# A decoder block on one core: first down-projection loads asked for in the last gate/up unit, residual added in the second group, last group in another order

## Chip, cores and metric

The kernel runs on one core of a Trainium2 chip. The metric is the device time of one execution in microseconds (us); the runs shown are three executions of the kernel before, and one more execution was profiled.

## What is computed

One hybrid decoder block in float32 on 1024 tokens of width 1024: a norm, an input projection, a state-space mixer and a retention mixer side by side, an output projection with a residual, and then the part that the change touches:

```python
h = rmsnorm(x, norm2_w[i])
a = jax.nn.silu(jnp.einsum("bsd,df->bsf", h, w_gate[i]))
u = jnp.einsum("bsd,df->bsf", h, w_up[i])
x = x + jnp.einsum("bsf,fd->bsd", a * u, w_down[i])
...
return rmsnorm(x, final_norm_w)
```

The inner width is 2816, which is 22 blocks of 128 or 11 pairs of blocks.

## The kernel before

Every float32 operand is split in two parts (`split`: ScalarE writes the rounded part, VectorE the rest), and each product is three TensorE matmuls of 128x128 by 128x512. The gate, up and down projections are done by Strassen's scheme in Winograd's form: two by two blocks need seven products, numbered 1 to 7, and each product goes into an accumulator in PSUM that several products share.

**Gate and up.** There are 22 units (class `Unit`), gate and up in turn for the 11 pairs. A unit runs its products in the order of `ORDER`, `(1, 5, 6, 2, 7, 3, 4)`; the first six units (`EARLY`) have done 1 and 2 beforehand and run `(5, 6, 7, 3, 4)`. The string `"XXYZYZZ"[i - 1]` names the accumulator of product i: 5 and 3 go to Y, and 6, 7 and 4 go to Z. After 5 and after 6 the accumulator is read out (`L989`: the tile `RS` for 6), before a later product is added on top. After the second unit of a pair, seven combinations of the result are split and stored to DRAM (`down_op`, `L1027`, tensors `aD`) through three staging buffers (the tile `x7` and two halves of `ktok`).

**Down.** The 11 pairs are taken in three groups of 4, 4 and 3 (`down_proj`), and each group runs seven products (class `Down`), one step for each pair in the group, 12 matmuls a step. The string `"1Z 5Y 6Z 3Y 7Z 2Y 4Z"` gives product and accumulator set (four PSUM banks each, one for each 128 tokens). A step needs two things: the stored combinations (`a`, loaded from `aD`, `L1160`) and a weight operand (`w`) made from raw rows of `w_down`: an even block (tile `qk`) and an odd block (tiles `m8` to `m11`), loaded at `L1152`. Product 5 makes a difference `t` of the halves of the even block, and later products change `t` with the odd block. `a` and `w` rotate over 20 tiles, `RING`: `m0`-`m3`, `m4`-`m7`, `h4`-`h7`, `m12`-`m15`, `h0`-`h3`. In gate/up these same tiles, with `qk`, hold the operands `B[1]` to `B[7]` of products 1 to 7: `B[1]` in `qk`, `B[5]` in `m0`-`m3`, `B[6]` in `m4`-`m7`, `B[2]` in `h4`-`h7`, `B[7]` in `m8`-`m11`, `B[3]` in `m12`-`m15` and `B[4]` in `h0`-`h3`.

After the last step of each product, `evac` adds each bank to its part of the result (`L1219`), tiles `x3[h, t]` (h a half of 512 tokens, t a tile of 128 of them), which have been loaded with the residual from `x2D` (`L1192`) at the first step of the first two products. In the last group `finish` makes the final norm: a sum of squares on ScalarE (`sumsq`), a reciprocal root by Newton steps of small VectorE instructions (`rsqrt1` for one column, `rsqrt` for several), the scaling, and the store to `out`.

**What sets the order.** Steps of gate/up and down stand in one list. At each step `advance` divides operands three steps ahead and calls `load` for steps further on; `at(i, f)` hangs a piece of work on step i. A list scheduler then orders each engine's program, with a higher priority for operand divisions and PSUM reads. All these loads and stores go through the one queue of SyncE (SP), which takes them in program order: an entry that waits for a tile to come free holds up what stands behind it.

Of the kernel before, what the change touches and what calls it, by code (L numbers as in the profile page):

```python
# [65 lines left out]
def block_kernel(ctx: ExitStack, tc: tile.TileContext, x, norm1_w, w_in, conv_w, conv_b,  # L66
# [858 lines left out]
    class Unit:  # L925
# [22 lines left out]
        def divide(self, k):  # L948
# [50 lines left out]
    def gate_up():  # L999
# [111 lines left out]
        for i, a in enumerate(todo):  # L1111
            u = Unit(*a, (5, 6, 7, 3, 4) if i < EARLY else Unit.ORDER)
# [14 lines left out]
    class Down:  # L1127
# [3 lines left out]
        def __init__(self, g, pos, i, bank_set, end):  # L1131

            self.b0, self.K = g
            self.pos, self.i, self.set, self.end = pos, i, bank_set, end
            self.n = down.setdefault("n", 0)
# [17 lines left out]

        def pair(self, j, k):
            return T([P, 2, 512], RING[4 * ((2 * self.n + j) % 5) + k], F32R)

        def divide(self, k):
            i = self.i
            self.a[k] = self.pair(0, k)
            nc.sync.dma_start(self.a[k].bitcast(F32), aD[self.b0 + k][i - 1])  # L1160
# [49 lines left out]
        def evac(self, t, ps):  # L1210
# [12 lines left out]
        def finish(self, h, b, t, xr):  # L1223
            if (h, b, self.i) == (0, 1, 3):
                if t == 0:
                    fin["ssq"] = T([P, NT, 2], "fq", bufs=2)
                sumsq(fin["ssq"][:, t, 1:2], xr)
            elif (h, b, self.i) == (0, 0, 2):
                sumsq(fin["ssq"][:, t, 0:1], xr)

                def f():
                    xr, ssq = x3[0, t], fin["ssq"]
                    s = T([P, 2], "fs", bufs=4)
                    tt(s[:, 0:1], ssq[:, t, 0:1], ssq[:, t, 1:2], op=ALU.add)
                    rsqrt1(s[:, 1:2], s[:, 0:1], 1.0 / DM, EPS)
                    stt(xr, xr, s[:, 1:2], wbf[0], op0=ALU.mult, op1=ALU.mult)  # L1236
                    nc.sync.dma_start(out[t * P:(t + 1) * P, :], xr)
                f()
            elif h == 1 and self.i in (7, 4):

                cs = slice(b * 512, (b + 1) * 512)
# [201 lines left out]
```

## Time and profile before

| | us |
|---|---|
| median of 3 runs (lowest, highest) | 1521.22 (1519.02, 1522.15) |
| profiled execution, its own time | 1519.29 |
| its span, first to last instruction | 1517.2 |
| TensorE busy | 1468.7 (97%) |
| VectorE busy | 1103.9 (73%) |
| ScalarE busy | 662.4 (44%) |
| moved by DMA | 257.41 MB, mean 170 GB/s |

Times in the trace count from the span's start. TensorE is the engine that is nearly always busy; so what matters is where it isn't, and what ends each of its waits. The time outside the span is 2.09 us.

### The profile page before, as it was taken

To read this page: it belongs to the slowest core of one execution; us is meant where nothing else is said; L and a number is where in the kernel's file an instruction comes from. 1 tells how busy PE (TensorE), PEld (TensorE's weight loads), DVE (VectorE), ACT (ScalarE), POOL (GpSimd) and SP (SyncE) were. 2 spreads that over 40 slices of the span, in tenths; PEclk is the share of its full clock that TensorE was granted. 3 is DMA by queue.
4 is the path that set the end of the run, shared out by engine and by line. 5 is a ranking of instruction groups with operands and counts; after the bars stand their busy time and mean duration, and the time that the engine had idled before them with its cause. 6 is when DMAs were issued, how large, how long until landed. Compare 5 with 4: busy or idle time off the path is not lost.

```text
span 1517.2 us, 20863 instructions
## 1 busy us (share of the span) xinstructions
PE 1468.7 (97%) x7278; PEld 1199.5 (79%) x7278; DVE 1103.9 (73%) x2321; ACT 662.4 (44%) x1280; POOL 36.0 (2%) x66
## 2 busy tenths in 40 slices
PE   9999999999999999999999999999999997799995
PEld 7888878888898878888888777888888886588884
DVE  5677898568688895677756889777777775565658
ACT  6344557435355665233545533444444442222223
POOL 1012000000000000000000000000000000000000
PEclk9999999999999999999999999999999999899997
DMA  7434555564434677655534355444444458877652
GB/s 238 111 92 107 160 181 174 162 196 116 114 100 130 186 214 235 202 167 156 184 117 120 119 173 187 153 153 147 145 152 145 147 210 322 296 257 234 206 167 111
DMA packets 142313, 257.41 MB, mean 170 GB/s; under 512 B 11332, under 2 KB 71552, under 8 KB 142208
## 3 DMA queue, kind: packets, MB, share of 16 engines
q1 hardware_dynamic: 141072, 254.66, 52.1%
q8 instruction: 57, 0.93, 0.3%
q10 hardware_dynamic: 736, 0.86, 0.2%
q0 software_dynamic: 400, 0.57, 0.1%
q14 instruction: 48, 0.39, 0.1%
HBM read 185.46 MB, written 70.58 MB: 169 GB/s over the span
## 4 chain that ended last, share of the span: by engine, by line
PE 92%; DVE 4%; DMA 2%; ACT 1%; issue 0%; SPq 0%; ACTq 0%
PE L L166 69%; PE M L166 21%; PE M L169 2%; DMA qk<-in_w_down_dram 0%; DMA x<-x2D 0%; DVE x L1219 0%; DMA m<-in_w_down_dram 0%; DMA wr<-in_w_in_dram 0%; DVE x L202 0%; DVE x L1236 0%; DMA aD<-x 0%; DVE nw L196 0%; DMA kc<-in_consts_dram 0%; DVE wp L202 0%; DVE m L202 0%
## 5 line engine op out<-in xcount | busy, mean ns | idle before, releaser
L166 PE MATMUL L<-h,wp 128*128 128x512 f32 x1128 | 272.6, 398 | 0.0
L255 DVE TENSOR_TENSOR wp<-wr,wp 128x512 fp32r<-128x512 f32 (+2 forms) x248 | 162.7, 656 | 145.0 <-ACT wp L254 140.0
L254 ACT ACTIVATE wp<-wr 128x512 fp32r<-128x512 f32 (+2 forms) x248 | 150.0, 605 | 263.4 <-PE L L166 216.3
L166 PE MATMUL L<-wp,h 128*128 128x512 f32 (+2 forms) x1248 | 260.1, 365 | 0.0
L166 PEld LDWEIGHTS L<-h,wp 128*128 128x128 f32 x1128 | 209.8, 188 | 50.7 <-issue 1.0
L166 PEld LDWEIGHTS L<-wp,h 128*128 128x128 f32 x1248 | 215.4, 188 | 30.6 <-issue 5.1
L166 PE MATMUL L<-wp,m 128*128 128x512 f32 x768 | 182.9, 396 | 0.0
L166 PEld LDWEIGHTS L<-wp,m 128*128 128x128 f32 x768 | 142.6, 188 | 32.9 <-issue 0.5
L166 PE MATMUL L<-m,wp 128*128 128x512 f32 x372 | 91.9, 395 | 0.9 <-DVE RS L989 0.9
L166 PE MATMUL L<-m,h 128*128 128x512 f32 x321 | 83.6, 404 | 7.5 <-ACT m L201 4.8
L166 PEld LDWEIGHTS L<-m,wp 128*128 128x128 f32 x372 | 69.7, 188 | 18.1 <-ACT x L201 1.3
L166 PEld LDWEIGHTS L<-m,h 128*128 128x128 f32 x321 | 60.7, 192 | 24.5 <-ACT m L201 5.6
L166 PE MATMUL L<-m,x 128*128 128x512 f32 x276 | 67.9, 394 | 1.8 <-DVE RS L989 1.8
L166 PEld LDWEIGHTS L<-m,x 128*128 128x128 f32 x276 | 51.6, 188 | 14.7 <-issue 2.6
L166 PE MATMUL M<-m,x 128*128 128x512 f32 x252 | 61.9, 394 | 1.0 <-ACT x L201 1.0
L166 PE MATMUL L<-h,m 128*128 128x512 f32 x216 | 55.5, 400 | 3.2 <-DVE x L1219 3.2
L166 PEld LDWEIGHTS M<-m,x 128*128 128x128 f32 x252 | 47.2, 188 | 12.5 <-ACT x L201 1.4
L398 DVE SCALAR_TENSOR_TENSOR m<-m,cols,m 128x512 f32<-128x512 f32 x72 | 52.2, 747 | 3.6 <-ACT m L396 3.3
L166 PEld LDWEIGHTS L<-h,m 128*128 128x128 f32 x216 | 41.3, 192 | 13.2 <-DVE x L1219 4.0
L166 PE MATMUL M<-m,m 128*64 128x128 f32 (+2 forms) x363 | 50.5, 301 | 0.0
L166 PE MATMUL L<-m,m 128*128 128x512 f32 x141 | 36.4, 403 | 8.2 <-ACT m L201 8.2
L201 ACT ACTIVATE m<-wp 128x512 fp32r<-128x512 f32 x29 | 18.3, 632 | 54.9 <-PE M L166 28.6
(333 smaller groups left out, 2365.0 us busy)
## 6 DMA issues: line engine op xcount, KB each, us to landing
wr<-in_w_in_dram SPq DMA_DIRECT2D x144, 256.0 KB, 2.8
aD<-ktok SPq DMA_DIRECT2D x49, 512.0 KB, 3.4
m<-aD SPq DMA_DIRECT2D x47, 512.0 KB, 4.0
wr<-in_w_out_dram SPq DMA_DIRECT2D x64, 256.0 KB, 2.9
h<-aD SPq DMA_DIRECT2D x30, 512.0 KB, 3.7
aD<-x SPq DMA_DIRECT2D x28, 512.0 KB, 3.7
x<-in_w_gate_dram SPq DMA_DIRECT2D x22, 512.0 KB, 3.8
x<-in_w_up_dram SPq DMA_DIRECT2D x22, 512.0 KB, 3.9
```

What stands on the lines that cost most here:

```text
L166: tc.keep_in_program_order(nc.tensor.matmul(o, a, b, start=start, stop=stop, **kw))
L169: tc.keep_in_program_order(nc.tensor.transpose(o, a, ident))
L201: a = act(pair[:, 0], src, AF.Copy).ins
L254: newest["act"] = act(pair[:, 0, :n], raw[:, :n], AF.Copy).ins
L255: newest["dve"] = tt(pair[:, 1, :n], raw[:, :n], pair[:, 0, :n].bitcast(F32), op=ALU.subtract).ins
L398: stt(dst, u[:, q:q + TH], w[q], dst, op0=ALU.mult, op1=ALU.add)
```

## The change

In the first six gate/up units product 6 goes before product 5. The first loads of the down-projection (even rows and `a` of the first product, `a` of the second, odd rows) are hung on the steps 7, 6, 4 and 3 before its first step, four at a time, instead of being called from `load` and `divide`; from the third product on, `load` asks for `a` too, which `divide` did before. The residual isn't loaded at the start any more: the first product to reach a part of the result is copied there by ScalarE, and during the second group the residual is loaded through two tiles in turn (`S` and `kcB`) and added by VectorE, eight additions of 128x1024. The last group runs product 2 first, loads its odd rows before its even rows, and normalises the first 512 tokens in one piece, hung on the step behind product 3; the second 512 tokens are normalised two tiles at a time.

```diff
@@ -953,12 +953,14 @@
-            if i == 5:
-                f = op["s1"] = T([P, 4, P], "wr", bufs=5)
-                tt(f, A21, A22, op=ALU.add)
-            elif i == 6:
-                f = stage["s2"]
-                tt(f, op.pop("s1"), A11, op=ALU.subtract)
+            if i in (5, 6):
+                f = op.pop("s1", None)
+                if f is None:
+                    f = op["s1"] = T([P, 4, P], "wr", bufs=5)
+                    tt(f, A21, A22, op=ALU.add)
+                if i == 6:
+                    s1, f = f, stage["s2"]
+                    tt(f, s1, A11, op=ALU.subtract)
...
-            u = Unit(*a, (5, 6, 7, 3, 4) if i < EARLY else Unit.ORDER)
+            u = Unit(*a, (6, 5, 7, 3, 4) if i < EARLY else Unit.ORDER)
...
-        def load(self, k):
+        def raw(self, k):
             if self.pos > 1:
                 return
-            r = (2 * (self.b0 + k) + self.pos) * P
-            if self.pos == 0:
+            odd = self.pos != self.swap
+            r = (2 * (self.b0 + k) + odd) * P
+            if not odd:
...
+        def acts(self, k):
+            self.a[k] = self.pair(0, k)
+            nc.sync.dma_start(self.a[k].bitcast(F32), aD[self.b0 + k][self.i - 1])
+
+        def load(self, k):
+
+            if self.n > 1:
+                self.raw(k)
+                self.acts(k)
...
                 if self.n in (0, 1):
-                    h = self.n
                     for t in range(NT):
-                        x3[h, t] = T([P, DM], f"x{4 * h + t}")
-                        nc.sync.dma_start(x3[h, t], x2D[h][t])
+                        x3[self.n, t] = T([P, DM], f"x{4 * self.n + t}")
...
+                if (h, b, t) not in down:
+                    down[h, b, t] = True
+                    copy(xr, ps)
+                    continue
                 tt(xr, ps, xr, op=ALU.add)
...
                 def f():
-                    xr, ssq = x3[0, t], fin["ssq"]
-                    s = T([P, 2], "fs", bufs=4)
-                    tt(s[:, 0:1], ssq[:, t, 0:1], ssq[:, t, 1:2], op=ALU.add)
-                    rsqrt1(s[:, 1:2], s[:, 0:1], 1.0 / DM, EPS)
-                    stt(xr, xr, s[:, 1:2], wbf[0], op0=ALU.mult, op1=ALU.mult)
-                    nc.sync.dma_start(out[t * P:(t + 1) * P, :], xr)
-                f()
+                    rs = T([P, NT], "rs", bufs=2)
+                    tt(rs, ssq[:, :, 0], ssq[:, :, 1], op=ALU.add)
+                    rsqrt(rs, rs, 1.0 / DM, EPS, NT)
+                    for q in range(NT):
+                        xr = x3[0, q]
+                        stt(xr, xr, rs[:, q:q + 1], wbf[0], op0=ALU.mult, op1=ALU.mult)
+                        nc.sync.dma_start(out[q * P:(q + 1) * P, :], xr)
+                at(self.last + 1, f)
...
+                elif t % 2:
+                    q = slice(t - 1, t + 1)
+                    stt(w[:, 0, q], w[:, 1, q], 1.0 / DM, w[:, 0, q], op0=ALU.mult, op1=ALU.add)
+                    rsqrt(w[:, 2, q], w[:, 0, q], 1.0, 0.0, 2)
+                    for t in (t - 1, t):
+                        xr, rs = x3[1, t], w[:, 2, t:t + 1]
+                        r = slice(TH + t * P, TH + (t + 1) * P)
+                        act(xr[:, 512:], xr[:, 512:], AF.Copy, scale=rs)
+                        nc.scalar.dma_start(out[r, 512:], xr[:, 512:])
+                        stt(xr[:, :512], xr[:, :512], rs, wbf[0][:, :512],
+                            op0=ALU.mult, op1=ALU.mult)
+                        nc.sync.dma_start(out[r, :512], xr[:, :512])
...
-        orders = "1Z 5Y 6Z 3Y 7Z 2Y 4Z", "5Y 1Z 3Y 6Z 2Y 7Z 4Y", "1Z 5Y 6Z 3Y 7Z 2Y 4Z"
-        return [Down(g, pos, int(o[0]), int(o[1] == "Y"), g == gs[2])
-                for g, os in zip(gs, orders) for pos, o in enumerate(os.split())]
+        orders = "1Z 5Y 6Z 3Y 7Z 2Y 4Z", "5Y 1Z 3Y 6Z 2Y 7Z 4Y", "2Y 1Z 5Y 6Z 3Y 7Z 4Z"
+        ds = [Down(g, pos, int(o[0]), int(o[1] == "Y"), g == gs[2])
+              for g, os in zip(gs, orders) for pos, o in enumerate(os.split())]
+        s0 = ds[0].first
+
+        def loads(f):
+            return lambda: [f(k) for k in range(4)]
+
+        for i, f in ((-7, ds[0].raw), (-6, ds[0].acts), (-4, ds[1].acts), (-3, ds[1].raw)):
+            at(s0 + i, loads(f))
...
+        for h in range(2):
+            for t in range(NT):
+                def f(h=h, t=t):
+                    a = down["res", h, t] = T([P, DM], ("S", "kcB")[t % 2])
+                    nc.sync.dma_start(a, x2D[h][t])
+
+                def g(h=h, t=t):
+                    tt(x3[h, t], x3[h, t], down["res", h, t], op=ALU.add)
+                at(ds[7].first + 3 * n, f)
+                at(ds[7].first + 3 * n + 5, g)
+                n += 1
+        return ds
```

The scheduler moves instructions on the engines, so three places are shown in its order. The first is SP's program where gate/up ends. Before, these twelve rows begin with the last two `a` loads of the first product (`m2`, `m3`); the one load of even rows that stands ahead of them is `qk` too, for the first step:

```order
L1160 DMA m2_1808_11561<-aD20_138 128x1024
L1160 DMA m3_1819_11596<-aD30_145 128x1024
L1160 DMA h4_1822_11619<-aD04_128 128x1024
L1160 DMA h5_1826_11643<-aD14_135 128x1024
L1160 DMA h6_1828_11669<-aD24_142 128x1024
L1160 DMA h7_1839_11700<-aD34_149 128x1024
L1160 DMA h3_1848_11778<-aD35_150 128x1024
L1160 DMA h0_1841_11718<-aD05_129 128x1024
L1160 DMA h1_1843_11736<-aD15_136 128x1024
L1160 DMA h2_1845_11758<-aD25_143 128x1024
L1160 DMA m4_1850_11796<-aD02_126 128x1024
L1152 DMA qk_1794_11466<-in_w_down_dram 128x1024
```

Now, at the same place:

```order
L1156 DMA qk_1789_11430<-in_w_down_dram 128x1024 x4
L1160 DMA m0_1792_11452<-aD00_124 128x1024
L1160 DMA m1_1793_11454<-aD10_131 128x1024
L1160 DMA m2_1794_11456<-aD20_138 128x1024
L1160 DMA m3_1795_11458<-aD30_145 128x1024
L1160 DMA h4_1803_11500<-aD04_128 128x1024
L1160 DMA h5_1804_11502<-aD14_135 128x1024
L1160 DMA h6_1805_11504<-aD24_142 128x1024
L1160 DMA h7_1806_11506<-aD34_149 128x1024
L1029 DMA aD100_194<-ktok_1284_8131 128x1024
L1156 DMA m8_1809_11529<-in_w_down_dram 128x1024
L1156 DMA m9_1810_11531<-in_w_down_dram 128x1024
```

The even rows of all four steps stand ahead of everything; before, those of the second step stood behind `a` loads into `h0`-`h3` (free after gate/up's last product) and `m4` (free after the down-projection's first step).

The second place is a little further on in SP's program, where now come the odd rows, the last stores of the gate/up pair (`aD`, written from `ktok` and `x7`) and the `a` loads of the third product (`h0`-`h3`) and of the fourth (`m4`):

```order
L1029 DMA aD103_197<-ktok_1284_8131 128x1024
L1029 DMA aD104_198<-x7_1285_8132 128x1024
L1029 DMA aD106_200<-ktok_1284_8131 128x1024
L1160 DMA h0_1830_11669<-aD05_129 128x1024
L1160 DMA h1_1841_11696<-aD15_136 128x1024
L1160 DMA h2_1843_11714<-aD25_143 128x1024
L1029 DMA aD105_199<-ktok_1284_8131 128x1024
L1029 DMA aD101_195<-x7_1285_8132 128x1024
L1029 DMA aD102_196<-ktok_1284_8131 128x1024
L1160 DMA h3_1845_11732<-aD35_150 128x1024
L1160 DMA m4_1847_11754<-aD02_126 128x1024
```

The last `a` of the third product stands behind the pair's last store; before, the `a` loads into `h0` to `h3` stood ahead of all these stores, as the first piece shows, and loads of `x2D` stood between the stores and the odd rows. No load of `x2D` stands here any more.

The third place is VectorE's program around the last product (4Z). Before, between the additions of its first and its second bank (`L1219` into `x4`, two rows above these, and into `x5`) stood:

```order
L196 TENSOR_SCALAR nw_2015_13106<-fs_2014_13104,nw_2015_13106 128x1
L1236 SCALAR_TENSOR_TENSOR x2_1816_11574<-x2_1816_11574,fs_2011_13083,wb0_1847_11776 128x1024
L197 TENSOR_SCALAR fs_2014_13104<-nw_2015_13106,fs_2014_13104 128x1
L1252 TENSOR_SCALAR mv_1990_12962<-mv_1990_12962 128x1
L196 TENSOR_SCALAR nw_2015_13106<-fs_2014_13104,nw_2015_13106 128x1
L1254 TENSOR_TENSOR S_1991_12963<-x4_1835_11680,wb0_1847_11776 128x512
L197 TENSOR_SCALAR fs_2014_13104<-nw_2015_13106,fs_2014_13104 128x1
L191 TENSOR_SCALAR nw_2019_13139<-mv_1990_12962 128x1
L192 TENSOR_SCALAR nw_2019_13139<-mv_1990_12962 128x1
L1236 SCALAR_TENSOR_TENSOR x3_1817_11576<-x3_1817_11576,fs_2014_13104,wb0_1847_11776 128x1024
L193 TENSOR_SCALAR nw_2019_13139<-nw_2019_13139 128x1
L1219 TENSOR_TENSOR x5_1836_11682<-L_1811_11567,x5_1836_11682 128x512
```

Now the four additions of the last product (`L1233`, tiles numbered 1837 to 1840) stand like this:

```order
L1233 TENSOR_TENSOR x_1837_11680<-L_11582,x_1837_11680 128x512
L1267 TENSOR_SCALAR mv_13069<-mv_13069 128x1
L1269 TENSOR_TENSOR x_1840_11683<-x_1840_11683,wb_1849_11772 128x512
L1233 TENSOR_TENSOR x_1838_11681<-L_11583,x_1838_11681 128x512
L1255 SCALAR_TENSOR_TENSOR x_1824_11588<-x_1824_11588,rs_13019,wb_1849_11772 128x1024
L1272 SCALAR_TENSOR_TENSOR mv_13069<-mv_13069 128x2
L1233 TENSOR_TENSOR x_1839_11682<-L_11584,x_1839_11682 128x512
L178 TENSOR_SCALAR nw_13127<-mv_13069 128x2
L1255 SCALAR_TENSOR_TENSOR x_1825_11589<-x_1825_11589,rs_13019,wb_1849_11772 128x1024
L179 TENSOR_SCALAR nw_13127<-nw_13127 128x2
L1233 TENSOR_TENSOR x_1840_11683<-M_11585,x_1840_11683 128x512
```

The scalings of the first 512 tokens (`L1255`, `L1236` before) still stand among them, two of the four; the reciprocal roots for those tokens have moved ahead of the last product.

## Rows read from the trace of the kernel before

A row of the first view has the stretch, its length, the busy us of PE, PEld, DVE, ACT and POOL with their instructions, the granted TensorE clock (1.00 is 2.4 GHz), the DMA share and GB/s. A row of a timeline has start, us, engine, line, operation, tiles, and in brackets the idle time before it and what ended that.

**Rows 1.** Busy time in four stretches: first group, second, rest, tail.

```profile
1258.00:1341.50 83.50, 64.02 (x242) 48.70 (x241) 45.78 (x73) 17.99 (x30) 0.61 (x1) 0.88 0.88 318
1341.50:1396.50 55.00, 55.00 (x241) 45.01 (x240) 32.14 (x52) 12.66 (x20) 0.00 (x0) 1.00 0.68 211
1396.50:1498.50 102.00, 102.00 (x445) 83.15 (x443) 65.71 (x142) 27.17 (x55) 0.00 (x0) 1.00 0.53 168
1498.50:1517.20 18.70, 0.05 (x1) 0.00 (x0) 14.75 (x60) 5.05 (x12) 0.00 (x0) 0.57 0.48 188
```

**Rows 2.** TensorE's waits in the whole span: us in total, times, longest.

```profile
PE L L166 <- ACT m L201: 13.1, 2, 8.2
PE L L166 <- DVE x L1219: 3.2, 1, 3.2
PE L L166 <- DVE RS L989: 2.6, 3, 0.9
PE M L166 <- DVE RS L989: 2.0, 2, 1.1
```

**Rows 3.** TensorE's timeline in the first early gate/up unit.

```profile
854.31 2.96 PE L166 MATMUL M<-m,wp 128*128 128x512 f32 x12
857.11 2.96 PE L166 MATMUL M<-m,x 128*128 128x512 f32 x12
861.15 3.04 PE L166 MATMUL M<-m,wp 128*128 128x512 f32 x12 [1.08 <-DVE RS L989]
```

**Rows 4.** SP's timeline where gate/up ends (duration over the merged issues).

```profile
1241.44 0.33 SPq L1152 DMA_DIRECT2D qk<-in_w_down_dram  x1
...
1247.73 10.78 SPq L1160 DMA_DIRECT2D h<-aD  x8
1260.91 0.32 SPq L1160 DMA_DIRECT2D m<-aD  x1
1261.28 0.42 SPq L1152 DMA_DIRECT2D qk<-in_w_down_dram  x1
```

**Rows 5.** The chain that ended last, pieces from 1255 to 1345 us.

```profile
1261.28 7.12 DMA qk<-in_w_down_dram
...
1290.87 5.73 DMA m<-in_w_down_dram
...
1311.42 5.85 DMA x<-x2D
```

**Rows 6.** TensorE's timeline at the starts of down products 1, 6 and 11.

```profile
1258.00 2.20 PE L166 MATMUL L<-m,m 128*128 128x512 f32 x9
...
1341.47 0.86 PE L166 MATMUL M<-m,m 128*128 128x512 f32 x3
...
1396.53 1.32 PE L166 MATMUL L<-m,m 128*128 128x512 f32 x5
```

**Rows 7.** ScalarE's timeline, the first even rows landed.

```profile
1245.69 0.63 ACT L201 ACTIVATE m<-qk 128x512 fp32r<-128x512 f32 x1 [0.84 <-DMA qk<-in_w_down_dram]
```

**Rows 8.** VectorE's timeline in an earlier reciprocal root, two chained instructions.

```profile
818.60 0.16 DVE L183 TENSOR_TENSOR nw<-rs,nw 128x4 f32<-128x4 f32 x1
818.80 0.17 DVE L184 TENSOR_TENSOR nw<-nw,rs 128x4 f32<-128x4 f32 x1
```

**Rows 9.** Timeline of the end, all engines.

```profile
1493.64 1.27 DVE L1236 SCALAR_TENSOR_TENSOR x<-x,fs,wb 128x1024 f32<-128x1024 f32 x1
...
1496.35 2.20 PE L166 MATMUL M<-m,m 128*128 128x512 f32 x9
...
1497.49 0.68 DVE L1219 TENSOR_TENSOR x<-L,x 128x512 f32<-128x512 f32 x1
...
1507.22 0.68 DVE L1219 TENSOR_TENSOR x<-M,x 128x512 f32<-128x512 f32 x1
...
1507.93 0.63 ACT L206 ACTIVATE u<-x 128x512 f32<-128x512 f32 x1 [1.12 <-DVE x L1219]
...
1513.56 0.35 ACTq L1261 DMA_DIRECT2D out_dram<-kcB  x1
```

More of the change, by code (lines that the diff above doesn't have):

```diff
@@ L1134, in __init__ @@
             self.pos, self.i, self.set, self.end = pos, i, bank_set, end
+            self.swap = int(end)
             self.n = down.setdefault("n", 0)
@@ L1158, in divide @@
             i = self.i
-            self.a[k] = self.pair(0, k)
-            nc.sync.dma_start(self.a[k].bitcast(F32), aD[self.b0 + k][i - 1])
             e, o = down["even"][:, k], down.get(("odd", k))
@@ L1223, in finish @@
         def finish(self, h, b, t, xr):
-            if (h, b, self.i) == (0, 1, 3):
+            if (h, b, self.i) == (0, 0, 1):
                 if t == 0:
                     fin["ssq"] = T([P, NT, 2], "fq", bufs=2)
-                sumsq(fin["ssq"][:, t, 1:2], xr)
-            elif (h, b, self.i) == (0, 0, 2):
                 sumsq(fin["ssq"][:, t, 0:1], xr)
-                def f():
-                    xr, ssq = x3[0, t], fin["ssq"]
-                    s = T([P, 2], "fs", bufs=4)
-                    tt(s[:, 0:1], ssq[:, t, 0:1], ssq[:, t, 1:2], op=ALU.add)
-                    rsqrt1(s[:, 1:2], s[:, 0:1], 1.0 / DM, EPS)
-                    stt(xr, xr, s[:, 1:2], wbf[0], op0=ALU.mult, op1=ALU.mult)
-                    nc.sync.dma_start(out[t * P:(t + 1) * P, :], xr)
-                f()
+            elif (h, b, self.i) == (0, 1, 3):
+                ssq = fin["ssq"]
+                sumsq(ssq[:, t, 1:2], xr)
+                if t < NT - 1:
+                    return
+                def f():
+                    rs = T([P, NT], "rs", bufs=2)
[6 more added lines that the diff above has]
+                at(self.last + 1, f)
             elif h == 1 and self.i in (7, 4):
-                cs = slice(b * 512, (b + 1) * 512)
                 if b:
@@ L1244, in finish @@
                         fin["w"] = T([P, 4, RH], "mv", bufs=2)
-                    if t == 1:
-                        fin["y"] = T([P, 2, DM], "ktok")
-                    fin[t] = fin["w"][:, t, :], (fin["y"][:, t - 1] if t in (1, 2) else
-                                                 T([P, DM], "kcB" if t else "S"))
-                w, y = fin[t]
-                sumsq(w[:, 1:2], xr)
-                ts(w[:, 0:1], w[:, 1:2], 1.0 / DM, EPS if b else w[:, 0:1],
-                   op0=ALU.mult, op1=ALU.add)
-                tt(y[:, cs], xr, wbf[0][:, cs], op=ALU.mult)
-                if b == 0:
-                    rsqrt1(w[:, 2:3], w[:, 0:1], 1.0, 0.0)
-                    r = slice(TH + t * P, TH + (t + 1) * P)
-                    ts(y[:, :640], y[:, :640], w[:, 2:3], None, op0=ALU.mult)
-                    nc.sync.dma_start(out[r, :640], y[:, :640])
-                    act(y[:, 640:], y[:, 640:], AF.Copy, scale=w[:, 2:3])
-                    nc.scalar.dma_start(out[r, 640:], y[:, 640:])
+                w = fin["w"]
+                sumsq(w[:, 1, t:t + 1], xr)
+                if b:
+                    ts(w[:, 0, t:t + 1], w[:, 1, t:t + 1], 1.0 / DM, EPS,
+                       op0=ALU.mult, op1=ALU.add)
+                    tt(xr, xr, wbf[0][:, 512:], op=ALU.mult)
+                elif t % 2:
[10 more added lines that the diff above has]
+                        nc.sync.dma_start(out[r, :512], xr[:, :512])
     def down_proj():
@@ L1266, in down_proj @@
         gs = (0, 4), (4, 4), (8, 3)
-        orders = "1Z 5Y 6Z 3Y 7Z 2Y 4Z", "5Y 1Z 3Y 6Z 2Y 7Z 4Y", "1Z 5Y 6Z 3Y 7Z 2Y 4Z"
-        return [Down(g, pos, int(o[0]), int(o[1] == "Y"), g == gs[2])
-                for g, os in zip(gs, orders) for pos, o in enumerate(os.split())]
+        orders = "1Z 5Y 6Z 3Y 7Z 2Y 4Z", "5Y 1Z 3Y 6Z 2Y 7Z 4Y", "2Y 1Z 5Y 6Z 3Y 7Z 4Z"
[6 more added lines that the diff above has]
+            at(s0 + i, loads(f))
+        n = 0
+        for h in range(2):
[9 more added lines that the diff above has]
+        return ds
     wbf, fin = [], {}
```

## The prediction

> **What bounds the kernel now.** I read the windows by stage first, then TensorE's waits, then the chain of waits and the timelines at the places that these name. TensorE bounds nearly all of the span. In the second group of the down-projection, and in the rest behind it, it is busy for the whole of each stretch at a granted clock of 1.00; in the first group it is busy for 64.02 of 83.50 us at a mean clock of 0.88, and in the last 18.70 us not at all [rows 1]. So there is time to win only where TensorE stands, and the change touches three such places.
>
> The waits say what it stands for: 13.1 us in two waits for operands that ScalarE splits, 3.2 us for a PSUM read that adds the residual, and 4.6 us in five short waits for the read into `RS` [rows 2]. ScalarE and VectorE aren't slow there; the chain goes past them to three DMAs: even rows that took 7.12 us, odd rows 5.73 us, and a load of the residual 5.85 us [rows 5]. The first of them was late because it was asked for late. SP issued the even rows of step 1 at 1241.44, then eight `a` loads between 1247.73 and 1258.5, then a load into `m4`, which comes free only in the down-projection's first step, and only then, at 1261.28, the even rows of step 2 [rows 4]. TensorE had begun at 1258.00 [rows 6] and needed them at about 1260.8.
>
> **Edit 1, products 6 and 5 exchanged in six units.** Before, 7 follows 6 directly and adds to the same accumulator, so it waits for VectorE to read 6 out. Product 6 began at 857.11 and 7 at 861.15, 4.04 us later, where 5 to 6 took 2.80 [rows 3]: 1.24 us lost, 0.16 more than the wait of 1.08. The five waits on `RS` have 4.6 us in all [rows 2], 0.92 each; with 0.16 added that is 1.08 a unit, and 6.5 us for six (the sixth unit has the same products; its wait is put down to ScalarE, a little later than the read). Now 5 lies between 6 and 7, and 7 between 5 and 3, so each read has a whole product, 2.80 us, for the 0.7 us that a read of 128x512 takes [rows 9]. Against it: 6's operand needs two VectorE sums where 5's needed one, 0.6 us more, and the division runs some three steps ahead. Bounds 0 (the operand late by as much as the read was) and 6.5 us; I take 6.0, near the whole, because a division three steps ahead has 8.4 us for those 0.6.
>
> The Trainium skill has a rule by which there would be more to win. "TensorE: Matmul & The Clock Gate", in "A second HAM failure mode: psum-queue depth-cycling", has small idles between matmul groups make the clock swing between its levels, so that more than the idle is lost. The matmuls after the first gap take their usual time, 3.04 against 2.96 us for twelve [rows 3], so the row doesn't bear it out. By the rule the edit would give back slow matmuls too, as in the second rival; by the rows it gives the 6.5 us alone.
>
> **Edit 2, the boundary.** The cost before is read off whole products. Five products, the 6th to the 10th, took 1396.53 - 1341.47 = 55.06 us without a gap; the first five took 1341.47 - 1258.00 = 83.47 [rows 6]. So 28.4 us were lost, of which 19.5 were idle and the rest slow matmuls after the idles (mean clock 0.88) [rows 1]. All three late DMAs are touched:
>
> - Even rows: all four are issued from 1241.4 on, when the tile `qk` comes free, one behind another. The first landed 4.2 us after its issue (1245.69) [rows 4, 7]. At the 318 GB/s that the DMAs gave in the first group [rows 1], half a MB takes 1.65 us, so the last lands at about 1250.7, 7 us ahead of need.
> - `a` of products 1 and 2, odd rows: issued as their tiles come free, the last after gate/up's second last products, at some 1253 us. Up to the last `a` of product 3, SP moves 4 + 4 + 4 + 4 + 4 loads and 7 stores, 27 x 0.524 MB = 14.2 MB; at 318 GB/s that is 44.5 us, done by 1286, and product 3's last step comes at 1258.0 + 2 x 11.0 + 8.3 = 1288.3. That is close, but 318 is a mean with standstills of SP in it.
> - The residual: the first product that reaches a result is now copied by ScalarE, which is busy 17.99 of 83.50 us [rows 1], and no PSUM read waits for `x2D`.
>
> What the moves cost. Behind SP's waiting entries stand the pair's stores and later `a` loads: `h3`'s load for product 3 is behind the last store, which waits for ScalarE, whose program has the reads of product 2's first two banks ahead of it. I work this out as: product 2 ends at 1280.1, split and store at about 1281.5, `h3` asked for at 1281.9, landed after 5.85 at most [rows 5], 1287.8, against 1288.3. In gate/up's last unit ScalarE stands for even rows 1 and 2 ahead of a PSUM read that product 7 needs at 1249.6; they land by 1245.7 and 1247.3, so 2 us of cover. I take 27.4 of the 28.4, 1 us for such remainders; the bounds are 28.4 and 20.
>
> The residual's eight additions of 128x1024 go to VectorE, at 1.27 us as for the scaling of that size [rows 9], 10.2 us; sixteen of its PSUM additions of 0.68 go to ScalarE, 10.9 us. In the second group VectorE is busy 32.14 of 55.00 us [rows 1], so there is room. Each addition stands five steps (13.8 us) behind its load's hook, more than any of the landings. If that cover were gone, VectorE would stand, and behind it the divisions and PSUM reads: this is the last rival.
>
> **Edit 3, the end.** Now TensorE ends at 1498.55, but VectorE adds the last bank only at 1507.22, 8.67 us late, because four scalings of 1.27 us and four reciprocal roots for the first tokens stand ahead of it. From that addition to the span's end it is another 9.98 us [rows 9]; together 18.65. In the new order the roots come before the last product, two of the scalings too, and the other two lie between additions while TensorE still works: I find the last addition 0.1 to 1.0 us behind the last matmul. Then: addition, square and its read-out, 1.5 us; about a dozen small instructions of the first pair of tiles woven with the second's, 1.2 to 2.4; two scalings of 0.6; seven chained instructions at 0.20 [rows 8], 1.4; two scalings, 1.2; and 3.64 us from the last store's issue at 1513.56 to the end [rows 9]. That is 10.1 to 11.3, so 10.2 to 12.3 after the last matmul; I take 11.6, the long side, since the root by pairs has 13 instructions where the single one had 10.
>
> Against it: 4Z now follows 7Z on the same banks, with no product between. "Perfetto Trace Analysis", under "Matmuls", in the Trainium skill asks for independent groups to turn through different banks, so that a read-out overlaps the next group; 7Z and 4Z break it. Worked out from rows: the roots (14 instructions at 0.20) and two scalings stand ahead of 7Z's first addition, which ends some 8.6 us after product 3's end, where 7Z ends at 8.3; so TensorE waits 0.4 us, 1.5 at most. If the read-out of each of the four banks stood in TensorE's way as in [rows 3], it would be 4 x 1.08 = 4.3 us, a rival below. Net gain of the end 18.65 - 11.6 - 0.4 = 6.6, bounds 4 and 8.
>
> **Sum.** 1519.29 of the profiled execution, its span of 1517.2 and 2.09 around it, less 6.0, 27.4 and 6.6, is 1479.3. That execution lies 1.9 us (0.13%) below the median of the three runs.
>
> **Rivals.**
> - A wait takes the place of those removed: SP's queue in its new order brings product 3's last `a` or product 4's first ones late, and TensorE stands once more with slow matmuls behind it. For it: the 0.5 us of cover above for `h3`, and three stores in a row. Against: the DMAs stand idle for some us before. Its price is the middle one of the old stalls, 5.73 us of landing [rows 5] and 3 us of slow matmuls (a third of the 8.9), 8.7 us: 1488.
> - Short gaps slow the matmuls behind them, so edit 1 returns more: 8.9 us of slow matmuls (28.4 - 19.5) for the three long stalls is 3 us each, 18 for six gaps, 1461. The 3.04 us behind the first gap [rows 3] speak against it. This is the clock rule of the Trainium skill's TensorE page, named above.
> - Edit 1 gives nothing, since the operand of 6 is late by what the read-out was: VectorE has five sums and splits to do for each unit there. 1485.
> - 7Z and 4Z on the same banks: TensorE waits at each of the four, 4.3 us instead of 0.4, 1483. Against it: the additions of banks 2 to 4 come 2.0 us apart or more in 4Z and take 0.68. It is the bank rule of the Trainium skill's trace page.
> - The edit of the end does not do what it says: the longer roots and the wait eat all of it. 1486.
> - Slower: an addition of the residual reaches VectorE before its load has landed, and since VectorE goes in order, divisions and reads stand behind it. SP holds a load until the addition two before has freed the tile. At the full landing of 5.85 us [rows 5] for each of eight, 46.8 us, if all of it reached TensorE: 1526. It decides when loads are issued less than 5.85 us ahead of their additions and the divisions have no lead; they have 13.8 us and 8.
>
> **Chances.** The forecast 0.62, with its own range 1474 to 1484. A new stall at product 3 or 4 0.15, edit 1 worth more 0.01, worth nothing 0.07, the banks 0.04, the end worth nothing 0.04, slower 0.03, and 0.04 for stalls adding up to between 1491 and 1522. The predicted time is 1479.3. The range takes in the rivals from 1483 to 1488 with a spread of runs of 2 to 3 us above them, and the low bound of the costs (6.5 + 28.4 + 8 off, 1476.4) less the same spread: 1474 to 1491. About 0.2%, 3 us, is what a measurement here can tell from no change; faster by more 0.95, within 0.02, slower 0.03.
>
> **What would show it.** Edit 1: no wait of TensorE for the `RS` read in the early units, starts 2.8 us apart. Edit 2: down products 1 to 5 in 55 to 57 us, the clock at 1.00 through gate/up's end, all four `qk` issues within 2 us of 1235. Edit 3: the last PSUM addition within 1 us of the last matmul, 11 to 12 us from there to the end. Wrong would be: idles of over 2 us in products 1 to 5, or VectorE standing for `x2D` in the second group.

## The result and the profile after

The changed kernel takes 1477.08 us, median of four runs. One of the four took 3721.12 us, for a reason that nothing here shows; it counts in that median but not in the ratio, and the other three (1476.39 to 1477.6) have a median of 1476.56. The runs of before beside them have a median of 1521.61; the ratio is 0.9709 (95% interval 0.969 to 0.9728). The forecast was 1479.3. The profiled execution took 1476.39 us with a span of 1474.6, against 1519.29 and 1517.2.

The windows of the changed kernel, in the columns of [rows 1]: six early units, first group up to product 6, tail.

```profile
853.80:937.90 84.10, 84.10 (x362) 67.47 (x362) 76.29 (x125) 33.24 (x57) 0.00 (x0) 1.00 0.50 169
1250.66:1305.71 55.05, 55.05 (x242) 45.05 (x241) 31.05 (x50) 21.33 (x36) 0.61 (x1) 1.00 0.94 365
1462.90:1474.60 11.70, 0.05 (x1) 0.00 (x0) 6.65 (x32) 3.39 (x6) 0.00 (x0) 0.72 0.63 240
```

TensorE is busy for the whole of the first two at a granted clock of 1.00, and the tail is 7 us shorter. All its waits in the whole span, which answer to [rows 2]:

```profile
PE M L166 <- DVE ones L112: 1.1, 1, 1.1
PE M L169 <- DVE m L202: 1.0, 1, 1.0
PE M L166 <- ACT qk L508: 0.8, 1, 0.8
PE L L166 <- ACT h L1378: 0.6, 2, 0.3
PE M L166 <- DVE h L903: 0.4, 1, 0.4
```

All lie ahead of the early units, the last at 845 us; none is at a place that the change touches. TensorE's timeline, of the early unit of [rows 3], of products 1 and 6, and of the last matmuls:

```profile
853.82 3.19 PE L166 MATMUL M<-m,wp 128*128 128x512 f32 x12
856.85 2.96 PE L166 MATMUL M<-m,x 128*128 128x512 f32 x12
859.64 2.97 PE L166 MATMUL M<-m,wp 128*128 128x512 f32 x12
...
937.85 2.96 PE L166 MATMUL L<-qk,wp 128*128 128x512 f32 x12
...
1250.66 2.20 PE L166 MATMUL L<-m,m 128*128 128x512 f32 x9
...
1305.71 1.54 PE L166 MATMUL M<-m,m 128*128 128x512 f32 x6
...
1460.75 2.20 PE L166 MATMUL M<-m,m 128*128 128x512 f32 x9
```

SP's timeline at the boundary, which answers to [rows 4]:

```profile
1234.10 1.76 SPq L1156 DMA_DIRECT2D qk<-in_w_down_dram  x4
1235.95 1.90 SPq L1160 DMA_DIRECT2D m<-aD  x4
1240.39 2.42 SPq L1160 DMA_DIRECT2D h<-aD  x4
1246.82 0.32 SPq L1029 DMA_DIRECT2D aD<-ktok  x1
1247.24 3.31 SPq L1156 DMA_DIRECT2D m<-in_w_down_dram  x4
...
1257.50 1.55 SPq L1160 DMA_DIRECT2D h<-aD  x3
1270.50 0.32 SPq L1029 DMA_DIRECT2D aD<-ktok  x1
...
1273.95 0.42 SPq L1160 DMA_DIRECT2D h<-aD  x1
```

The four loads of even rows are issued together; before, 20 us lay between the first and the second. The last two rows that the prediction spoke of are VectorE's last PSUM addition, 0.21 us behind the last matmul's end (1460.75 + 2.20), and the last stores:

```profile
1463.16 0.68 DVE L1233 TENSOR_TENSOR x<-M,x 128x512 f32<-128x512 f32 x1
...
1469.28 0.98 ACTq L1278 DMA_DIRECT2D out_dram<-x  x2
```

Where the 42.6 us of span went, from starts of the same instruction in both traces:

| stretch | before | after | gain |
|---|---|---|---|
| early units | 854.31 to 945.08 = 90.77 | 853.82 to 937.85 = 84.03 | 6.74 |
| from there to product 1 | 312.92 | 312.81 | 0.11 |
| down products 1 to 5 | 83.47 | 55.05 | 28.42 |
| product 6 to the last matmul's end | 157.08 | 157.24 | -0.16 |
| tail | 18.65 | 11.65 | 7.00 |

The 0.49 left lie ahead of the early units.

### The profile page after: what moved, and what is told of

Its sections match the earlier page's. It is cut to its first block, busy times and chain, and to the rows that moved or that the text cites. A ratio compares the mean times of both kernels' runs of the same rounds, so it can differ in the third digit from the quotient of the medians.

```text
span 1474.6 us, 20840 instructions
## 1 busy us (share of the span) xinstructions
PE 1459.0 (99%) x7278; PEld 1196.9 (81%) x7278; DVE 1093.7 (74%) x2263; ACT 670.8 (45%) x1296; POOL 36.5 (2%) x66
## 4 chain that ended last, share of the span: by engine, by line
PE 96%; DVE 2%; ACT 1%; DMA 1%; issue 0%; DVEq 0%; ACTq 0%
PE L L166 72%; PE M L166 22%; PE M L169 2%; DVE x L1233 0%; DMA wr<-in_w_in_dram 0%; DVE x L1255 0%; DMA kc<-in_consts_dram 0%; DVE x L1269 0%; DVE x L1279 0%; DVE m L202 0%; ACT m L201 0%; ACT x L455 0%; ACT u L206 0%; DVE nw L183 0%; ACT m L638 0%
## 5 line engine op out<-in xcount | busy, mean ns | idle before, releaser
L166 PE MATMUL L<-m,wp 128*128 128x512 f32 x360 | 88.9, 395 | 0.0
L166 PE MATMUL L<-m,h 128*128 128x512 f32 x321 | 80.4, 395 | 0.7 <-ACT h L1378 0.6
L166 PE MATMUL M<-m,x 128*128 128x512 f32 x240 | 58.9, 394 | 0.0
L166 PE MATMUL L<-h,m 128*128 128x512 f32 x207 | 52.0, 392 | 0.0
L166 PE MATMUL L<-h,x 128*128 128x512 f32 x180 | 44.6, 396 | 0.0
L166 PE MATMUL M<-m,wp 128*128 128x512 f32 x168 | 41.7, 396 | 0.0
```

What stands on the lines that cost most here:

```text
L166: tc.keep_in_program_order(nc.tensor.matmul(o, a, b, start=start, stop=stop, **kw))
```

## Experiments

Each kernel was timed beside the kernel before on the same chip. "P1-5" is the time from the start of down product 1 to that of product 6. Differences in the text are between medians, where the runs of one changed kernel spread over 0.7 to 3.5 us, or between the traces of one execution each, where it says so.

| kernel | median us | ratio to before, 95% | P1-5, us |
|---|---|---|---|
| before | 1521.61 | | 83.47 |
| changed | 1477.08 | 0.9709, 0.969 to 0.9728 | 55.05 |
| e1_early_5_6 | 1484.6 | 0.9757, 0.9743 to 0.9772 | 55.05 |
| e2_swap_alone | 1515.12 | 0.9955, 0.994 to 0.9971 | 85.57 |
| e3_loads_late | 1482.43 | 0.9745, 0.9731 to 0.976 | 60.77 |
| e4_residual_back | 1488.34 | 0.9784, 0.9769 to 0.9798 | 66.64 |
| e10_a_in_divide | 1500.07 | 0.9855, 0.984 to 0.9869 | 77.78 |
| e11_a_in_load_alone | 1485.93 | 0.9765, 0.9749 to 0.9781 | 62.92 |
| e12_early_and_divide | 1497.08 | 0.9843, 0.9826 to 0.986 | 74.32 |
| e7_add_at_once | 1477.95 | 0.9712, 0.9697 to 0.9726 | 55.05 |
| e5_old_end | 1483.75 | 0.9756, 0.974 to 0.9773 | 55.05 |
| e6_order_alone | 1481.58 | 0.9737, 0.9723 to 0.9752 | 55.05 |
| e9_short_tail | 1476.57 | 0.9704, 0.969 to 0.9719 | 55.05 |
| e13_half_scaled_early | 1477.06 | 0.9709, 0.9696 to 0.9722 | 55.05 |

P1-5 is 55.05 in every run that leaves the loads of edit 2 up to there as they are, so the other edits have no part in it there.

### Edit 1: e1_early_5_6, e2_swap_alone

The first undoes the exchange in the changed kernel; the second makes it alone in the kernel before, with the lines of `divide` from the change.

```diff
-            u = Unit(*a, (6, 5, 7, 3, 4) if i < EARLY else Unit.ORDER)
+            u = Unit(*a, (5, 6, 7, 3, 4) if i < EARLY else Unit.ORDER)
```

> The changed kernel with edit 1 alone undone: the six early units take their products as 5, 6, 7, 3, 4 again. If the exchange is worth what the two traces show between the first early product and the next kind of unit (90.77 against 84.03 us), this kernel is 6.7 us slower than the changed one, about 1483.8 us; TensorE waits some 0.9 us for the read into RS in each early unit, and its granted clock stays at 1.00 there. If short gaps slow the matmuls behind them, the clock in that stretch falls below 1.00 and the loss is well over 7 us. If the gain of that stretch came from elsewhere in the change, the time stays within 1 us of 1477.

Measured: 7.5 us slower than the changed kernel. TensorE's waits in its early units, and the window of that stretch:

```profile
PE M L166 <- DVE RS L991: 2.8, 3, 1.1
PE L L166 <- DVE RS L991: 2.6, 3, 0.9
```

```profile
853.77:944.48 90.71, 85.25 (x362) 67.12 (x360) 78.55 (x128) 33.68 (x57) 0.00 (x0) 1.00 0.50 174
```

The stretch is 6.68 us longer, 90.71 against 84.03, with six waits of 0.9 to 1.1 us (the sixth is shown as the `RS` read here). They are 5.4 us of idle time together; the other 1.3 us are lost though the clock stays at 1.00 behind all six.

> The kernel before with edit 1 alone: products 6, 5, 7, 3, 4 in the six early units. If the 6.7 us of that stretch are its own, the time is 1514.8 us beside 1521.5, with no wait of TensorE for the read into RS there and down products 1 to 5 in 83 us as before. If the earlier start of what follows is lost again at the boundary, because the loads there hang on times that do not move, the down products take longer and the gain is below 3 us.

Measured: 6.3 us between the medians, near the first case; between the two profiled executions it is 3.07 us (1516.22 against 1519.29). Its early units took 84.65 us (855.69 to 940.34), 6.1 less than before, with no wait for the read into `RS`, but its first five down products 85.57, 2.1 more than before. So in that execution a part was lost again at the boundary; the size lies near the spread of runs.

### Edit 2: early loads, residual, and the place of the activation loads

`e3_loads_late` takes out the four hooks and loads step by step; `e4_residual_back` loads `x2D` at the start of products 1 and 2 and adds it at every PSUM read.

```diff
-        for i, f in ((-7, ds[0].raw), (-6, ds[0].acts), (-4, ds[1].acts), (-3, ds[1].raw)):
-            at(s0 + i, loads(f))
...
-            if self.n > 1:
-                self.raw(k)
-                self.acts(k)
+            self.raw(k)
+            self.acts(k)
```

```diff
+                        nc.sync.dma_start(x3[self.n, t], x2D[self.n][t])
...
-                if (h, b, t) not in down:
-                    down[h, b, t] = True
-                    copy(xr, ps)
-                    continue
...
-                at(ds[7].first + 3 * n, f)
-                at(ds[7].first + 3 * n + 5, g)
```

> The changed kernel with the weight and activation loads of the first two down products asked for step by step again, as before; the residual stays in the second group. If the late weights were two of the three stalls, they come back: 13.1 us of waiting for operands that ScalarE splits and two thirds of the 8.9 us of slow matmuls, 6, so 19 us more, about 1496. If a first stall only hid behind the others and all of the 28.4 us were theirs, 1505. If the residual's loads in the queue were what made the weights late, 1477 to 1480.

> The changed kernel with the residual loaded at the start of products 1 and 2 again and added by VectorE at each read of PSUM; the early loads stay. If the residual was the third stall by itself, TensorE waits 3.2 us for the read of PSUM and a third of the slow matmuls comes back, 3 us: about 1483. If the residual was late only because the weights were late, its loads now find a free queue and the time stays within 1 us of 1477. If its eight loads of half a MB push later activation loads back in SP's queue, more than 8 us: over 1485.

Measured: 5.4 and 11.3 us slower than the changed kernel. e3 missed all of its cases, the first by 14 us; for the residual the last case, over 1485, came true. The only wait of TensorE in the first group is for an activation load, in e3 at product 2's last step and in e4 at product 3's second. From TensorE's timeline of e3, then of e4:

```profile
1272.56 2.90 PE L166 MATMUL M<-m,h 128*128 128x512 f32 x6 [2.74 <-DMA h<-aD]
```

```profile
1285.49 4.18 PE L166 MATMUL L<-m,h 128*128 128x512 f32 x9 [8.83 <-DMA h<-aD]
```

SP's timeline of e4 says why:

```profile
1259.13 0.32 SPq L1160 DMA_DIRECT2D h<-aD  x1
1260.04 1.62 SPq L1203 DMA_DIRECT2D x<-x2D  x2
1274.38 0.32 SPq L1029 DMA_DIRECT2D aD<-ktok  x1
...
1277.96 1.26 SPq L1203 DMA_DIRECT2D x<-x2D  x2
1279.28 1.58 SPq L1160 DMA_DIRECT2D h<-aD  x3
```

SP stands for the pair's store until 1274.38, as it does in the changed kernel until 1270.50. There, three of product 3's four `h` loads are ahead of that store; here only one is, and the other three come behind it and two more loads of `x2D`.

In e3 all four even rows were issued from 1233.81 to 1237.03, without any hook. So something else had held them before. The diff moves the activation load out of `divide`, which is emitted at high priority, into `load`, which isn't. Two runs set that apart, and a third keeps the early loads but puts it back from product 3 on:

```diff
             i = self.i
+            self.acts(k)
             e, o = down["even"][:, k], down.get(("odd", k))
```

In `e10_a_in_divide` this stands with late loads and the moved residual; in `e12_early_and_divide` under `if self.n > 1`, with the early loads; `e11_a_in_load_alone` joins the edits of e3 and e4, so that of edit 2 only the new place of the activation loads is left.

> The changed kernel without the early loads, and with each down step's activation load back inside the division, which is emitted at high priority, so that on SP's queue nine of them stand between the first and the second load of even rows, as before; the residual stays in the second group. If that order of the queue is what made the even rows late, 13.1 us of waiting and 6 us of slow matmuls come back or more: 1496 to 1505 us. If the early loads are what removed the stalls, the place of the activation loads is worth nothing beside them and the time is that of the run with late loads, 1482.

> The changed kernel without the early loads and with the residual loaded and added in products 1 and 2, as before, but the activation loads outside the division. Of the kernel before, edit 2 is then undone but for that. If the place of the activation loads alone removes the wait for even rows, the loss stays below the 28.4 us of before: the sum of the two single losses, 5.4 for late loads and 11.3 for the residual, gives 1494; if both were one wait for the same activation load behind SP's entries, 1489. If their place is worth nothing, 1505.

> The changed kernel with its early loads of the first two products, but from the third product on with the activation load back inside the division, at high priority. In the program's order some fourteen of these loads then stand on SP's queue ahead of the odd rows of products 1 to 7. If the queue's order decides, the even rows are on time but the odd rows are late, and TensorE stands before the first product that needs them, the third: two of the three stalls and their slow matmuls, 10 to 20 us, 1487 to 1497. If the early loads alone cure the boundary, the time stays within 2 us of 1477.

Measured: 1500.07, 1485.93 and 1497.08. The first and the last are what the order of the queue would give; e11 lost less than either of its sums. SP's timeline of e10 has the picture of [rows 4] again, though the residual is gone:

```profile
1235.86 0.33 SPq L1156 DMA_DIRECT2D qk<-in_w_down_dram  x1
1236.56 2.42 SPq L1160 DMA_DIRECT2D m<-aD  x4
1242.15 10.78 SPq L1160 DMA_DIRECT2D h<-aD  x8
1255.33 0.32 SPq L1160 DMA_DIRECT2D m<-aD  x1
1255.70 0.42 SPq L1156 DMA_DIRECT2D qk<-in_w_down_dram  x1
```

Thirteen activation loads stand between the first and the second load of even rows, and TensorE waits 8.91 us there:

```profile
1264.21 4.03 PE L166 MATMUL L<-m,m 128*128 128x512 f32 x9 [8.91 <-ACT m L201]
```

In e11 the four even rows were issued from 1235.01 to 1238.17, though no hook asks for them, and TensorE waits only for activation loads, in products 2 and 3:

```profile
1266.23 1.67 PE L166 MATMUL M<-m,h 128*128 128x512 f32 x6 [0.81 <-DMA h<-aD]
...
1271.70 2.51 PE L166 MATMUL M<-m,h 128*128 128x512 f32 x6 [2.40 <-DMA h<-aD]
...
1284.16 2.32 PE L166 MATMUL L<-m,h 128*128 128x512 f32 x9 [2.33 <-DMA h<-aD]
```

In e12 the even rows are early, but the odd rows stand behind the overtaking loads until 1275.20 (1247.24 in the changed kernel), and TensorE waits in products 3 and 4, the second time for ScalarE's read of PSUM, which stood behind a store of the pair. From the timelines of SP and TensorE:

```profile
1275.20 2.05 SPq L1156 DMA_DIRECT2D m<-in_w_down_dram  x4
...
1281.38 0.79 PE L166 MATMUL L<-m,h 128*128 128x512 f32 x1 [6.57 <-ACT m L201]
...
1304.15 1.65 PE L166 MATMUL L<-h,m 128*128 128x512 f32 x3 [6.63 <-ACT x L172]
```

From P1-5: of the 28.42 us, the place of the activation loads gives 20.55 by itself (83.47 to 62.92). The moved residual gives 5.69 without it (77.78), and residual and early loads together 9.15 (74.32, with the activation loads of products 1 and 2 early too). These three runs have edit 1 as well; counted from the 85.57 of e2, which has it too, the gains are 2.10 larger. Two pairs of runs differ in nothing but the place: e10 and e3 (77.78 against 60.77, 17.01 us) and e12 and the changed kernel (74.32 against 55.05, 19.27 us). With the new place, early loads and residual give the other 7.87 between them; and early loads with the old residual are worse than neither (66.64 against 62.92).

Two things are not set apart. `load` is called up to three steps further ahead than `divide`, so the place changes the step as well as the priority; that the priority decides follows from the code, since the loads now come later on the queue though they are asked for earlier, but no run changes it alone. And in e11 the DMAs were busy for all of P1-5 (share 1.00, 384 GB/s; 0.94 and 365 in the changed kernel), so a part of what the moved residual gives may come from the four loads of `x2D`, 2.1 MB, that it takes out of this stretch, and not from the order of the queue.

### The additions of the residual: e7_add_at_once

```diff
-                    tt(x3[h, t], x3[h, t], down["res", h, t], op=ALU.add)
-                at(ds[7].first + 3 * n + 5, g)
+                    with tc.high_priority(PRIO):
+                        tt(x3[h, t], x3[h, t], down["res", h, t], op=ALU.add)
+                at(ds[7].first + 3 * n, g)
```

> The changed kernel with each addition of the residual placed at high priority right behind its load, instead of five steps behind it at low priority, so that VectorE stands until the load has landed. Eight landings of up to 6 us follow one another three steps, 8.3 us, apart. If the divisions' lead of some 8 us covers each stand, the time stays within 3 us of 1477. If each stand reaches TensorE, up to 46.8 us: 1523, the case that the prediction priced as slower than before.

Measured: 1477.95, no difference that can be told. But the run doesn't test what it was made for: VectorE never stood for `x2D`. The first load was issued at 1311.76 and its addition came at 1324.36, and between load and addition of the eight pairs lay 6.4 to 17.6 us, though both have the same step. The price of that rival stays open.

### Edit 3: e5_old_end, e6_order_alone

e5 has the order and the finish of before; e6 the new order, and the finish of before by single tiles.

```diff
-        orders = ..., "2Y 1Z 5Y 6Z 3Y 7Z 4Z"
+        orders = ..., "1Z 5Y 6Z 3Y 7Z 2Y 4Z"
```

> The changed kernel with the last group in its former order and with its former finish. If edit 3 is worth what the traces show behind the last matmul (18.65 against 11.65 us), this kernel is 7.0 us slower, about 1484; the last PSUM addition comes some 8.7 us behind the last matmul again. If 7 and 4 on the same banks cost the changed kernel something that no wait shows, the loss is less than 7 and the products of the last group are shorter here. If the end gains nothing, 1477.

> The changed kernel with the new order of the last group, but the former finish, which takes the reciprocal root of each tile by itself. If the order is what brings the last PSUM addition back to the last matmul, it comes within 1 to 3 us of it, the old 9.98 us follow, and the time is 1477 to 1479. If roots taken for four and two tiles at once are what saves time, 1480 to 1484.

Measured: e5 is 6.7 us slower, as expected; its last matmul ends at 1463.47 and its span at 1482.1, a tail of 18.63. e6 is 4.5 us slower, the case of the roots; its last PSUM addition comes 4.30 us behind the last matmul, not 1 to 3. Its timeline:

```profile
1459.23 0.68 DVE L1233 TENSOR_TENSOR x<-L,x 128x512 f32<-128x512 f32 x1
...
1460.02 6.40 PE L166 MATMUL L<-m,m 128*128 128x512 f32 x27 [2.17 <-issue]
...
1466.25 2.20 PE L166 MATMUL M<-m,m 128*128 128x512 f32 x9
...
1472.75 0.68 DVE L1233 TENSOR_TENSOR x<-M,x 128x512 f32<-128x512 f32 x1
```

Product 4 starts 0.11 us after the first addition of 7 ends (1459.23 + 0.68), and TensorE stands 2.17 us for it. The trace names no releaser, but product 4 adds to the same banks, and in the changed kernel it starts 0.11 us after that addition too (1453.72 + 0.68, and 1454.51), there only 0.08 us later than its pace. With roots tile by tile VectorE is late, the tail is 13.55 (1482.0 less 1468.45), 1.90 more than in the changed kernel, and the stand comes on top. So the order alone gives 5.1 us of tail (18.63 to 13.55) and loses 2.17 to the stand; the roots by four and by two give 1.90 of the tail and nearly all of the stand back, 4.0 of the 4.5 us between the medians. The Trainium skill ("Perfetto Trace Analysis", under "Matmuls") asks for independent groups to turn through different banks, so that a read-out overlaps the next group. Products 7 and 4 aren't independent, but with another product between them, as before, the read-out had that time: e6 agrees with the rule, and the changed kernel pays almost nothing, since its first read-out is in time.

### A shorter end: e9_short_tail, e13_half_scaled_early

Both multiply the first tokens' first half by the weight after product 1, so that ScalarE can scale it; e9 also takes the last product's roots tile by tile.

```diff
                 sumsq(fin["ssq"][:, t, 0:1], xr)
+                tt(xr, xr, wbf[0][:, :512], op=ALU.mult)
...
-                        stt(xr, xr, rs[:, q:q + 1], wbf[0], op0=ALU.mult, op1=ALU.mult)
+                        act(xr[:, :512], xr[:, :512], AF.Copy, scale=rs[:, q:q + 1])
+                        stt(xr[:, 512:], xr[:, 512:], rs[:, q:q + 1], wbf[0][:, 512:],
+                            op0=ALU.mult, op1=ALU.mult)
```

> The changed kernel with a shorter end: the first tokens' half that is complete after product 1 is multiplied by the weight there, so that ScalarE scales it and VectorE only the other half; and the last product's roots are taken tile by tile with ten instructions each, not by pairs, so that nothing of the third tile stands ahead of the last one's chain. If VectorE's queue sets the end, the last tile's ten chained instructions at 0.20 and one scaling of 0.68 follow its sum of squares, the last store is issued some 2 us earlier and the span ends 9 to 10 us behind the last matmul instead of 11.65: 1474 to 1475. If the landing of the last stores sets it, or the more numerous small instructions crowd VectorE, 1476 to 1478.

> The changed kernel with the first tokens' first half multiplied by the weight already after product 1, so that at the end ScalarE scales that half and VectorE only the other, at 0.68 instead of 1.27 us a tile; the roots stay by four and by two tiles. VectorE's order then has only one scaling between the additions, eleven of the first pair's thirteen root instructions ahead of the last addition, and the first pair's scalings while ScalarE squares the last tile. If VectorE's queue sets the end, the second pair's root is ready about 1.0 us earlier and the span ends 10.6 us behind the last matmul instead of 11.65: about 1476. If the landing of the stores sets it, 11.65 and 1477. The difference is near what a comparison of times can tell; the tail in the trace decides.

Measured: 1476.57 and 1477.06. The tails are 11.16 and 11.06 us, half a us shorter, which no comparison of times here can tell. In e9 a scaling and small instructions of earlier tiles stand ahead of the last addition, which comes at 1465.52, 2.08 us behind the last matmul (1463.44). e13's tail lies between its two cases, 10.6 and 11.65. Neither beats the changed kernel by what can be measured, and what sets the rest of the tail stays open.

## Why the prediction was right, and where its reasons were not

- **Edit 1**, 6.0 forecast, 6.74 in the trace, 6.68 undone in e1. The mechanism was the one given; the size is a little above its upper bound of 6.5, since a gap cost 1.11 us (6.68 / 6), not 1.08. The clock rule of the Trainium skill ("TensorE: Matmul & The Clock Gate", in "A second HAM failure mode: psum-queue depth-cycling"), as the prediction took it, would have had the six gaps slow the clock; e1 has the gaps, and 1.00 behind them. That section of the Trainium skill speaks of idles that come frequently enough, without a number; so e1 speaks only of gaps like these, one in each 15 us.
- **Edit 2**, 27.4 forecast, 28.42 measured. The size was right because the first five products could only fall to the pace of the next five. The reason was incomplete. The prediction saw in [rows 4] that the even rows stood behind `a` loads (it names nine; with the four into `m0` to `m3` it is thirteen), but it gave the cure to loads that are asked for earlier and a residual that is read later, and did not ask why the `a` loads stood ahead. They overtook, by the code, because `divide` is emitted at high priority; taking them out gives 20.55 of the 28.42 (e11), and without that both other parts together give 9.15 (e12). So 27.4 came out nearly right for the change as a whole, and would have been far off for the two parts that the prediction credited. The three stalls were not three separate prices either: e3, e4 and e11 show one queue, in which each part shifts the wait to the next activation load.
- **The first rival**, a late activation load of product 3 at 8.7 us, did not happen, but it is what e4 shows, at 11.59 us (66.64 - 55.05). The cover was larger than worked out: `h3` was asked for at 1273.95 (forecast 1281.9, less the 7.3 us by which all is earlier, 1274.6), landed 4.8 us later, and was needed at 1280.93: 2.2 us, not 0.5.
- **The residual's additions** did not keep the 13.8 us behind their loads that the step distance promised. They were moved back to gaps in VectorE's program, and the loads with them, since each waits for a free tile: the load of 1363.77 was issued 0.02 us after the addition before it on that tile (1362.53 + 1.22). The closest pair in the changed kernel is 5.5 us apart, and VectorE stood once; from the timelines of SP and VectorE:

```profile
1363.77 0.32 SPq L1304 DMA_DIRECT2D S<-x2D  x1
...
1369.29 1.22 DVE L1307 TENSOR_TENSOR x<-x,S 128x1024 f32<-128x1024 f32 x1 [1.45 <-DMA S<-x2D]
```

  VectorE standing for `x2D` in the second group is one of the two signs of being wrong that the prediction named, and it is there, at 1.45 us of its last rival's 46.8. TensorE did not wait. The step distance was wrong as a measure of cover. That the divisions' lead took up the 1.45 us fits, but no run tests what a longer stand would cost.
- **Edit 3**, 6.6 forecast, 7.00 in the tail less 0.08 of waiting. The tail of 11.65 was forecast as 11.6; the wait of 0.4 for 7Z was oversized. The rival with a stand at each of four banks didn't come: the last matmuls run without a gap.
- The sum missed by 2.9 us (1476.39 against 1479.3 for the profiled execution): 0.7 in edit 1, 1.0 in edit 2, 0.4 in edit 3, 0.5 ahead of the early units, 0.3 outside the span.

## What to carry to other kernels

When a load is late on a queue that goes in order, read what stands ahead of it and ask who put it there: an operation that is emitted at high priority takes its loads along, and these may wait for tiles that come free much later than those of the loads that they overtake. Where a change has several parts for one stall, undo them one by one and together, since what they give does not add up: here the moved activation load gave more than the early loads and the moved residual together. How far a wait is covered is read from issue and use in the trace, not from the distance in program steps.

## What the hardware showed

A stand of TensorE costs more than its idle time, but not in proportion to it. Windows behind the 2.74 us in e3, behind the 8.83 us in e4, and behind the 0.81, 2.40 and 2.33 us in e11 (columns as in [rows 1]):

```profile
1272.50:1275.20 2.70, 2.64 (x6) 2.15 (x7) 0.00 (x0) 0.60 (x1) 0.00 (x0) 0.50 1.02 405
```

```profile
1285.50:1289.50 4.00, 4.00 (x10) 3.13 (x11) 0.00 (x0) 0.00 (x0) 0.00 (x0) 0.50 1.03 416
```

```profile
1266.20:1268.00 1.80, 1.77 (x8) 1.45 (x9) 1.80 (x4) 0.63 (x1) 0.00 (x0) 1.00 1.01 407
1271.70:1274.20 2.50, 2.50 (x7) 1.96 (x8) 1.79 (x4) 0.00 (x0) 0.00 (x0) 0.59 1.03 419
1284.10:1286.50 2.40, 2.33 (x10) 1.97 (x11) 0.32 (x1) 0.00 (x0) 0.00 (x0) 1.00 1.03 411
```

At 0.50 the clock is at its lower level, 1.2 GHz. P1-5 is longer by the idle and by 2.98 us in e3 (60.77 - 55.05 - 2.74) and 2.76 in e4 (66.64 - 55.05 - 8.83). In e11 the three stands cost 2.33 us together beyond their idle time (62.92 - 55.05 - 5.54), and the clock fell behind one of them only, the 2.40. So in these three runs the prediction's price of 3 us of slow matmuls goes by falls of the clock, 2.3 to 3.0 us for one, and not by stands. Why it fell behind 2.40 us and not behind 2.33 is left open, and the six gaps of e1 left it at 1.00.
